# Expert slots weighted one at a time, key choices cut into pieces, and gathered rows in the weight ring

## The chip, the cores and the metric

One core of one Trainium2 chip runs the whole program in one launch. The metric is the time of the program on the device in microseconds, the median of the runs shown; smaller is better.

## What is computed

A first block (two hybrid layers) and a second block (two layers) follow each other on 256 tokens of width 1024. The change concerns the second block, whose layer is this:

```python
xn = rmsnorm(x, norm_mix[l])
proj = xn @ w_in[l]                      # five mixers read slices of it
cat = rmsnorm(cat, group_norm[l])        # the mixers' outputs
x = x + cat @ w_out[l]
x = x + peer_ffn(rmsnorm(x, norm_ffn[l]), peer_wq[l], peer_subkeys[l], peer_u[l], peer_v[l])

def peer_ffn(xn, wq, subkeys, u_tab, v_tab):
    q = (xn @ wq).reshape(b, s, 8, 2, 128)
    sc = einsum('bshjc,hjkc->bshjk', q, subkeys)
    top_s, top_i = top_k(sc, 16)
    cand = top_s[..., 0, :, None] + top_s[..., 1, None, :]
    best, ci = top_k(cand, 16)
    idx = i1 * 128 + i2                  # which of 16384 experts
    g = softmax(best)
    act = gelu(einsum('ckd,cd->ck', u_tab[idx], xn))
    y = einsum('ck,ckd->cd', g * act, v_tab[idx])
```

Each token takes 8 heads x 16 = 128 experts. An expert is a row of 2048 floats, u beside v, in one table in HBM.

## The kernel before

Tokens lie in two tiles of 128 (`tt` 0 and 1). `second` (L1424) runs for each layer `mix2` (five mixers, then `down`, the product with w_out), then `peer`. The program is built with the tile framework's scheduler, which may move an engine's instructions past each other; `issue_after` keeps a step from being placed before a given instruction. Each engine then runs its own list strictly in order.

**Weights.** `unit` (L196) loads 1 MB into one of three `raw` buffers of the ring (L188) and splits it in two halves: ScalarE rounds to `hi` (L212), VectorE or GpSimd makes `lo = raw - hi` (L216). A product is three matmuls (L236).

**The expert stage.** `peer` (L1248) first takes in the mixers' output (`arrive`, L1256: the sum, the gain, the transposes), projects head 0 and 1 for tile 0 (`project`, L1298) and chooses experts (`route`, L1321: `top16` by VectorE's max, index and replace instructions, then index arithmetic, some 35 VectorE instructions a head and tile, and one exponential on ScalarE). Then come 256 *slots*: 16 for each of 8 heads, first all of tile 0 ("first half"), then all of tile 1 ("second half"). For a slot, GpSimd issues an indirect DMA (L1377) that gathers 128 rows of 8 KB, 1 MB, into one of 8 `uv` buffers; VectorE multiplies the u half with the token and sums (L1379, the *dot*); ScalarE makes the gelu (L1383), VectorE multiplies by the gate (L1384), ScalarE scales an identity by the weight (L1387, `dgw`), and TensorE adds the weighted v half into two PSUM banks (L1389, two matmuls that the profile shows as four records). Then the buffer is free for the gather eight slots later. Four slots form a group: one gelu and one gate product for four weights.

```python
for i in range(GROUP):
    ... indirect_dma_start(out=r, ...)                     # L1377
    dots.append(... scalar_tensor_tensor(..., accum_out=act[:, i:i + 1]))
nc.scalar.activation(wt, act, AF.Gelu, scale=rs[tt])       # 128 x 4
nc.vector.tensor_tensor(wt, wt, gate[:, tt, h, k0:k0 + GROUP], op=OP.mult)
for i, r in enumerate(rows):
    nc.scalar.activation(dg, self.ident, AF.Copy, scale=wt[:, i:i + 1])
    for half in range(2): nc.tensor.matmul(y[tt][half], dg, r[:, ...])
```

The rest of the layer's routing is put between the groups by a list `todo`: the second token tile's `arrive`, the projections of heads 2 to 7 (each brings a wq unit), and a `route` for each head and tile. Each is one step, which the scheduler may then spread. After `peer`, `add_rms` (L1234) adds the result, normalizes and transposes for the next layer, whose first product (`attention(0)` in `mix2`, tile `p_s2`) begins.

Of the kernel before, what the change touches and what calls it, by code (L numbers as in the profile page):

```python
# [47 lines left out]
GROUP = 4  # L48
# [127 lines left out]
class _Kernel:  # L176
# [75 lines left out]
    def toks_first(self, outs, ws, xt):  # L252

        for tt in range(NT):
            k0, n = 0, sum(len(w[0]) for w in ws)
            for w in ws:
                for k in range(len(w[0])):
                    self.mm3(outs[tt], [t[:, tt, k0] for t in xt], [t[k] for t in w], k0 == 0, k0 == n - 1)
                    k0 += 1
# [140 lines left out]
    def down(self, y, unit, n, lhs, at, places=(None, None), parts=2):  # L400
# [561 lines left out]
    def mix2(self, l, x, xt):  # L962
# [33 lines left out]
        def attention(c):  # L996
            p = [self.bank([512], "acc", "p_s2") for _ in range(NT)]
            self.toks_first(p, [self.unit(a["win2_s"][l, c, kh], 4, 512, 8 if c == 0 else 0) for kh in range(2)], xt)
# [150 lines left out]
        self.down(y, lambda b, **k: self.unit(a["wout2"][l, order[b]], 2, D, LO, **k), len(order),  # L1149
                  lambda b: self.cat[order[b]], lambda b: 0, (None, place))  # L1150
# [95 lines left out]
    def peer(self, l, x, xt, y_in):  # L1246
# [9 lines left out]
        def arrive(tt):  # L1256
# [4 lines left out]
            for i in range(2):  # L1261
# [3 lines left out]
                self.transposed(xg[tt][:, sl], KT // 2, xt, tt, k0=i * KT // 2)  # L1265
            for i in range(2):
# [54 lines left out]
        def route(tt, h):  # L1321
# [14 lines left out]
            top16(c, best, ci)  # L1336
            ids = W.tile([P, 2, TOPK], F32, tag="ids", name="ids", bufs=2)
# [12 lines left out]
            nc.vector.tensor_tensor(cf, cf, i1, op=OP.subtract)  # L1350
            for j, (pos, out) in enumerate(((ab, i1), (cf, i2))):
# [15 lines left out]
            return last  # L1367
# [3 lines left out]
        def experts(tt, h, k0):  # L1371

            rows = []
            act = W.tile([P, GROUP], F32, tag="act", name="act", bufs=3)
            for i in range(GROUP):
                r = uv.pop(0) if uv else W.tile([P, 2 * D], F32, tag="uv", name="uv", bufs=GBUFS)
                nc.gpsimd.indirect_dma_start(out=r, out_offset=None, in_=a["puv"],  # L1377
                                             in_offset=bass.IndirectOffsetOnAxis(ap=idx[:, tt, h, k0 + i:k0 + i + 1], axis=0))
                dots.append(nc.vector.scalar_tensor_tensor(r[:, :D], r[:, :D], 1.0, xg[tt], op0=OP.mult, op1=OP.mult,  # L1379
                                                           accum_out=act[:, i:i + 1]))  # L1380
                rows.append(r)
            wt = W.tile([P, GROUP], F32, tag="wt", name="wt", bufs=3)
            nc.scalar.activation(wt, act, AF.Gelu, scale=rs[tt])  # L1383
            nc.vector.tensor_tensor(wt, wt, gate[:, tt, h, k0:k0 + GROUP], op=OP.mult)  # L1384
            for i, r in enumerate(rows):
                dg = W.tile([P, P], F32, tag="dgw", name="dgw", bufs=4)
                nc.scalar.activation(dg, self.ident, AF.Copy, scale=wt[:, i:i + 1])  # L1387
                for half in range(2):
                    nc.tensor.matmul(y[tt][half], dg, r[:, D + 512 * half:D + 512 * half + 512],  # L1389
                                     start=h == 0 and k0 + i == 0, stop=h == HEADS - 1 and k0 + i == TOPK - 1)  # L1390


        weights(0)
        arrive(0)
        project(0, 0, 1)
        dots = [route(0, 0)]
        weights(1)
        project(1, 0, 1)

        def late():  # L1400
            arrive(1)
            if l + 1 < L:
# [11 lines left out]
        for n, (tt, h) in enumerate([(tt, h) for tt in range(NT) for h in range(HEADS)]):  # L1414
            for k0 in range(0, TOPK, GROUP):
                while todo and todo[0][0] <= TOPK * n + k0:
                    step = todo.pop(0)[1]
                    with self.tc.issue_after(dots[-1].ins):
                        step()
                experts(tt, h, k0)  # L1420
# [57 lines left out]
```

## Time and profile before

| | |
|---|---|
| median of 3 runs | 3249.17 us (3243.63 to 3259.98) |
| profiled execution, its own time | 3238.84 us |
| span of its instructions | 3237.1 us |
| TensorE busy | 87% of the span |
| VectorE, ScalarE, GpSimd busy | 66%, 37%, 27% |
| mean granted TensorE clock | 0.94 |
| bytes moved by DMA | 841.78 MB, mean 260 GB/s |
| software DMA queue (the gathers) | 536.90 MB |
| expert gathers issued, first and last of layer 0 | 1606.99 us, 2327.01 us |
| expert gathers issued, first and last of layer 1 | 2515.05 us, 3213.80 us |

The shares are averages over stages with different limits, so the page's total says little: the span is to be read in stretches. A 40-slice strip on the page and the views by stretch give each stretch its busy engines, its granted clock and what the DMA engines moved. A wait in brackets behind an instruction is the idle time of its engine just before, and what ended it.

### The profile page before, as it was taken

How to read it: one execution, taken by the hardware profiler on the slowest of the kernel's cores; microseconds unless marked ns; L12 is line 12 of the kernel's file. 1: busy time of each engine (PE TensorE's matmuls, PEld its weight loads, DVE VectorE, ACT ScalarE, POOL GpSimd, SP SyncE). 2: the span in 40 equal slices, each digit the busy share in tenths (PEclk: the TensorE clock that was granted, in tenths of full speed). 3: DMA queues.
4: the chain of work that ended last, by engine and by line, in shares of the span. 5: the costliest groups of instructions: out<-in, count | busy, mean ns of one | idle time of the engine just before them, and what ended most of it. 6: DMA issues, size and time to landing. Idle time of an engine off the chain costs nothing.

```text
span 3237.1 us, 39712 instructions
## 1 busy us (share of the span) xinstructions
PE 2814.0 (87%) x13968; PEld 2058.1 (64%) x13968; DVE 2131.9 (66%) x4974; ACT 1199.3 (37%) x2300; POOL 882.7 (27%) x628
## 2 busy tenths in 40 slices
PE   9999999999999999999788877777889688867777
PEld 9988988989988988978644433332377344323333
DVE  6568667565577567569766676666487666766664
ACT  5446344445445344436432222212164322222121
POOL 0013221011023220011234454434311444444343
PEclk9999999999999999999889988888899899898889
DMA  6554235555553344554399999999843899999998
GB/s 256 183 187 158 100 122 202 183 182 213 182 189 135 105 156 176 182 184 144 129 379 397 391 371 365 397 378 374 344 146 108 347 391 376 378 399 384 379 376 353
DMA packets 121734, 841.78 MB, mean 260 GB/s; under 512 B 14016, under 2 KB 16832, under 8 KB 22208
## 3 DMA queue, kind: packets, MB, share of 16 engines
q0 software_dynamic: 73728, 536.90, 41.4%
q1 hardware_dynamic: 47520, 301.82, 26.2%
q8 instruction: 111, 1.82, 0.2%
q14 instruction: 87, 0.71, 0.1%
q10 hardware_dynamic: 288, 0.52, 0.0%
HBM read 838.15 MB, written 1.05 MB: 259 GB/s over the span
## 4 chain that ended last, share of the span: by engine, by line
PE 46%; DMA 19%; DVE 17%; issue 9%; POOL 6%; ACT 2%; POOLq 0%; DVEq 0%; SPq 0%; ACTq 0%
DMA uv<-in_puv_dram,idx 19%; PE p_gu L236 14%; PE p_y L236 10%; POOL uv L1377 6%; DVE uv L1379 4%; PE p_g L236 4%; PE p_y L1389 3%; PE p_b L236 2%; PE p_c L236 2%; PE p_gx L236 2%; DVE conv L542 1%; DVE lo L216 1%; PE p_tr L293 1%; PE p_s L236 1%; ACT hi L212 1%
## 5 line engine op out<-in xcount | busy, mean ns | idle before, releaser
L1389 PE MATMUL p_y<-uv,dgw 128*128 128x512 f32 x2048 | 1024.9, 659 | 295.8 <-ACT dgw L1387 295.8
L1389 PEld LDWEIGHTS p_y<-uv,dgw 128*128 128x128 f32 x2048 | 423.5, 212 | 866.5 <-issue 498.8
L1379 DVE SCALAR_TENSOR_TENSOR uv<-uv,xg 128x1024 f32<-128x1024 f32 x512 | 632.6, 1237 | 479.4 <-DMA uv<-in_puv_dram,idx 448.4
L1377 POOL DMA_INDIRECT uv<-in_puv_dram,idx x512 | 603.1, 1178 | 870.9 <-PE p_y L1389 508.3
L216 DVE TENSOR_TENSOR lo<-raw,hi 128x1024 fp32r<-128x1024 f32 (+1 forms) x390 | 480.7, 1236 | 311.9 <-ACT hi L212 309.9
L212 ACT CAST hi<-raw 128x1024 fp32r<-128x1024 f32 (+1 forms) x500 | 513.8, 1034 | 449.4 <-PE p_gu L236 125.1
L216 POOL TENSOR_TENSOR lo<-raw,hi 128x1024 fp32r<-128x1024 f32 (+1 forms) x110 | 274.4, 2500 | 1446.6 <-ACT hi L212 860.1
L236 PE MATMUL p_gu<-xt,hi 128*128 128x256 f32 x2560 | 463.6, 283 | 0.0
L236 PEld LDWEIGHTS p_gu<-xt,hi 128*128 128x128 f32 x2560 | 399.6, 192 | 0.0
L236 PE MATMUL p_gu<-xt,lo 128*128 128x256 f32 x1280 | 362.5, 283 | 0.0
L1383 ACT ACTIVATE wt<-act,rms_r 128x4 f32<-128x4 f32 x128 | 38.1, 297 | 848.2 <-DVE uv L1379 848.1
L236 PEld LDWEIGHTS p_gu<-xt,lo 128*128 128x128 f32 x1280 | 245.7, 192 | 0.0
L1387 ACT ACTIVATE dgw<-ident,wt 128x128 f32<-128x128 f32 x512 | 165.6, 391 | 77.6 <-DVE wt L1384 65.3
L236 PE MATMUL p_c<-xt,hi 128*128 128x256 f32 x960 | 182.6, 290 | 0.4 <-ACT sh L1095 0.4
L236 PE MATMUL p_y<-hi,ht 128*128 128x512 f32 x576 | 181.2, 395 | 0.0
L236 PEld LDWEIGHTS p_c<-xt,hi 128*128 128x128 f32 x960 | 152.9, 194 | 2.4 <-ACT sh L1095 1.1
L236 PE MATMUL p_c<-xt,lo 128*128 128x256 f32 x480 | 138.2, 289 | 0.0
L236 PE MATMUL p_y<-lo,ht 128*128 128x512 f32 x320 | 126.3, 395 | 0.0
L236 PE MATMUL p_g<-hi,xt 128*128 128x512 f32 x384 | 125.1, 399 | 0.0
L236 PEld LDWEIGHTS p_y<-hi,ht 128*128 128x128 f32 x576 | 108.5, 188 | 25.1
L236 PEld LDWEIGHTS p_c<-xt,lo 128*128 128x128 f32 x480 | 92.9, 194 | 0.2
L236 PE MATMUL p_g<-lo,xt 128*128 128x512 f32 x192 | 77.3, 403 | 8.2 <-DVE lo L216 7.0
(517 smaller groups left out, 3953.0 us busy)
## 6 DMA issues: line engine op xcount, KB each, us to landing
raw<-in_gu_dram SPq DMA_DIRECT2D x86, 1024.0 KB, 4.8
raw<-in_dn_dram SPq DMA_DIRECT2D x44, 1024.0 KB, 4.8
raw<-in_win_t_dram SPq DMA_DIRECT2D x30, 1024.0 KB, 4.9
raw<-in_win_g_dram SPq DMA_DIRECT2D x24, 1024.0 KB, 4.8
raw<-in_wout_dram SPq DMA_DIRECT2D x18, 1024.0 KB, 4.9
raw<-in_wq_dram SPq DMA_DIRECT2D x16, 1024.0 KB, 4.9
raw<-in_wbr_dram SPq DMA_DIRECT2D x12, 1024.0 KB, 4.8
raw<-in_win_s_dram SPq DMA_DIRECT2D x8, 1024.0 KB, 8.1
```

Of the source, the lines that this page charges most:

```text
L212: self.nc.scalar.copy(hi, r)
L216: engine.tensor_tensor(lo[:, a:b], r[:, a:b], hi[:, a:b].bitcast(F32), op=OP.subtract)
L236: self.nc.tensor.matmul(out, A[i], B[j], start=first and n == 0, stop=last and n == 2)
L293: nc.tensor.transpose(p[:, j], x[:, (g + j) * P:(g + j + 1) * P], self.ident)
L542: nc.vector.scalar_tensor_tensor(c[:, s:], th[:, j, :T - s], pc[:, 4 * f + 3 - s:4 * f + 4 - s], c[:, s:], op0=OP.mult, op1=OP.add)
L1377: nc.gpsimd.indirect_dma_start(out=r, out_offset=None, in_=a["puv"], in_offset=bass.IndirectOffsetOnAxis(ap=idx[:, tt, h, k0 + i:k0 + i + ...
L1379: dots.append(nc.vector.scalar_tensor_tensor(r[:, :D], r[:, :D], 1.0, xg[tt], op0=OP.mult, op1=OP.mult, accum_out=act[:, i:i + 1]))
L1383: nc.scalar.activation(wt, act, AF.Gelu, scale=rs[tt])
L1387: nc.scalar.activation(dg, self.ident, AF.Copy, scale=wt[:, i:i + 1])
L1389: nc.tensor.matmul(y[tt][half], dg, r[:, D + 512 * half:D + 512 * half + 512], start=h == 0 and k0 + i == 0, stop=h == HEADS - 1 and k0 + ...
```

## The change

- Each slot has its own gelu (128 x 1); the product with the gate moves from VectorE to ScalarE (a Copy with the gate as its scale); the groups of four are gone, and with them the VectorE product.
- `route` and `arrive` become generators that yield between pieces (six pieces a `route`). Behind every dot, `beside` lets one piece of the first due step run. The due slots move a little (for tile 1 from 24 to 20 slots ahead). The choice of head 1, tile 0, is made before the first slot.
- In the second half, slots 0, 4 and 7 of every 11 gather into the ring's three `raw` buffers instead of a `uv` buffer, in layer 0 up to slot 107 of 128, in layer 1 to the end.
- wq's first unit is asked for inside `down`, before the last products of the mixers (`then`), and not in `peer`.
- The next layer's `add_rms` for tile 0, its two first units and the first product for tile 0 are written as a step due at slot 228 (`following`), and `attention(0)` goes on from there.

```diff
@@ down, mix2
         last = [(m + i, unit(m + i, place=place, parts=parts)) for i, place in enumerate(places)]
+        if then:
+            then()
...
+        def then():
+            self.wq0 = self.unit(a["wq"][l, 0], KT, 2 * P)
@@ attention
+            if c == 0 and l:
+                ws, p0 = self.begun
+                p = [p0, self.bank([512], "acc", "p_s2")]
+                self.tile_toks(p[1], ws, xt, 1)
@@ route
             for j in range(2):
                 top16(sc[:, j], tv[:, j], ti[:, j])
+                yield
...
             top16(c, best, ci)
+            yield
...
             nc.vector.tensor_tensor(cf, cf, i1, op=OP.subtract)
+            yield
...
                 nc.vector.tensor_reduce(out, e, axis=AX.X, op=OP.add)
+                if j == 0:
+                    yield
@@ expert (was experts, by groups)
+        def expert(tt, h, k):
+            n = TOPK * h + k
+            if uv:
+                r = uv.pop(0)
+            elif tt == NT - 1 and n % 11 in (0, 4, 7) and n < (108 if l + 1 < L else 128):
+                r = self.ring.tile([P, 2 * D], F32, tag="raw", name="raw", bufs=3)
+            else:
+                r = W.tile([P, 2 * D], F32, tag="uv", name="uv", bufs=GBUFS)
...
+            dot = nc.vector.scalar_tensor_tensor(r[:, :D], r[:, :D], 1.0, xg[tt], ..., accum_out=act)
+            dots.append(dot)
+            beside(dot)
             nc.scalar.activation(wt, act, AF.Gelu, scale=rs[tt])
-            nc.vector.tensor_tensor(wt, wt, gate[:, tt, h, k0:k0 + GROUP], op=OP.mult)
+            nc.scalar.activation(wt, wt, AF.Copy, scale=gate[:, tt, h, k:k + 1])
+            dg = W.tile([P, P], F32, tag="dgw", name="dgw", bufs=4)
+            nc.scalar.activation(dg, self.ident, AF.Copy, scale=wt)
@@ following
+        def following():
+            self.next_xt = self.xt_tiles()
+            self.add_rms(x, y, self.next_xt, 0)
+            yield
+            ws = []
+            for kh in range(2):
+                ws.append(self.unit(a["win2_s"][l + 1, 0, kh], 4, 512))
+                yield
+            p = self.bank([512], "acc", "p_s2")
+            self.tile_toks(p, ws, self.next_xt, 0)
+            self.begun = ws, p
+            yield
@@ the list of steps
-            todo.append((TOPK * (HEADS + h) - 24, lambda h=h: route(1, h)))
+            todo.append((TOPK * (HEADS + h) - 20, route(1, h)))
+        if l + 1 < L:
+            todo.append((TOPK * (2 * HEADS - 2) + 4, following()))
...
+        def beside(dot):
+            if todo and todo[0][0] <= len(dots) - 2:
+                with self.tc.issue_after(dot.ins):
+                    while todo and next(todo[0][1], todo) is todo:
+                        todo.pop(0)
```

How the built programs' instructions stand, at three places. An x at a row's end counts repeats.

ScalarE in the first half of layer 0, about slots 16 to 23 (`act` holds dots, `wt` the weights, `dgw` the scaled identity). Before:

```order
L1383 ACTIVATE wt<-act,rms_r 128x4
L1387 ACTIVATE dgw<-ident,wt 128x128 x4
L1383 ACTIVATE wt<-act,rms_r 128x4
L1387 ACTIVATE dgw<-ident,wt 128x128 x4
L1383 ACTIVATE wt<-act,rms_r 128x4
```

Now:

```order
L1406 ACTIVATE wt<-act,rms_r 128x1
L1407 ACTIVATE wt<-wt,gate_15641 128x1
L1409 ACTIVATE dgw<-ident,wt 128x128
L1406 ACTIVATE wt<-act,rms_r 128x1
L1407 ACTIVATE wt<-wt,gate_15641 128x1
L1409 ACTIVATE dgw<-ident,wt 128x128
```

A weight waits for one dot and not for four, and VectorE is no longer between gelu and `dgw`.

VectorE at the same place, where the choice of head 2 begins. Before:

```order
L1379 SCALAR_TENSOR_TENSOR uv,act<-uv,xg_15635 128x1024 x4
L1275 MAX tv<-sc 128x8 x2
L1276 MAX_INDEX ti<-tv,sc 128x8
L1384 TENSOR_TENSOR wt<-wt,gate_15631 128x4
L1276 MAX_INDEX ti<-tv,sc 128x8
L1332 TENSOR_TENSOR cand<-tv 128x24
L1277 MATCH_REPLACE sc<-tv,sc 128x128 x2
L1278 MAX tv<-sc 128x8 x2
L1279 MAX_INDEX ti<-tv,sc 128x8
L1332 TENSOR_TENSOR cand<-tv 128x36
L1379 SCALAR_TENSOR_TENSOR uv,act<-uv,xg_15635 128x1024
```

Now:

```order
L1403 SCALAR_TENSOR_TENSOR uv,act<-uv,xg_15645 128x1024 x8
L1288 MAX tv<-sc 128x8
L1289 MAX_INDEX ti<-tv,sc 128x8
L1290 MATCH_REPLACE sc<-tv,sc 128x128
L1291 MAX tv<-sc 128x8
L1292 MAX_INDEX ti<-tv,sc 128x8
L1403 SCALAR_TENSOR_TENSOR uv,act<-uv,xg_15645 128x1024
L1288 MAX tv<-sc 128x8
L1289 MAX_INDEX ti<-tv,sc 128x8
```

The scheduler had put dots between the instructions of a choice already, at places of its own; now there is a dot after every piece.

VectorE between the mixers' last product and the experts of layer 0 (`p_y` is that product, `xg` the input times the gain, the second `lo` rows the first wq units). Before:

```order
L216 TENSOR_TENSOR lo<-raw,hi 128x1024 x2
L1263 TENSOR_TENSOR x_74<-p_y,x_74 128x512 x2
L296 TENSOR_TENSOR cat_1_15402<-p_tr,cat_0_15401 128x256
L216 TENSOR_TENSOR lo<-raw,hi 128x1024 x2
L1264 TENSOR_TENSOR xg_15635<-x_74,gain 128x512 x2
```

Now:

```order
L215 TENSOR_TENSOR lo<-raw,hi 128x1024 x2
L1275 TENSOR_TENSOR x_74<-p_y,x_74 128x512 x2
L298 TENSOR_TENSOR cat_1_15402<-p_tr,cat_0_15401 128x256
L215 TENSOR_TENSOR lo<-raw,hi 128x1024 x2
L1276 TENSOR_TENSOR xg_15645<-x_74,gain 128x512 x2
```

Nothing moved here but the line numbers; TensorE, ScalarE and SyncE stand as before up to the first slot too. The four `lo` of the next layer's first two units, on GpSimd behind gathers 96 and 100 of layer 0 before, are VectorE's now, behind dot 231. The next layer's `add_rms` for tile 0 and its product `p_s2` stood behind dot 131 of layer 0 before (the scheduler had drawn them forward) and stand behind dots 229 to 231 now.

## Rows read from the trace of the kernel before

**Rows 1.** The page's strip of 40 slices of the span: DMA share in tenths, GB/s.

```profile
DMA  6554235555553344554399999999843899999998
GB/s 256 183 187 158 100 122 202 183 182 213 182 189 135 105 156 176 182 184 144 129 379 397 391 371 365 397 378 374 344 146 108 347 391 376 378 399 384 379 376 353
```

**Rows 2.** Busy time by stretch of the expert stages; last columns clock, DMA share, GB/s.

```profile
core 0: us, PE busy (x) PEld busy (x) DVE busy (x) ACT busy (x) POOL busy (x), PEclk, DMA share, GB/s
1612.00:2332.00 720.00, 561.75 (x1431) 265.02 (x1432) 459.19 (x1310) 173.03 (x424) 308.16 (x256) 0.87 0.96 383
...
2523.00:3220.00 697.00, 538.06 (x1402) 253.70 (x1403) 446.76 (x1292) 165.92 (x413) 294.28 (x250) 0.90 0.96 388
3160.00:3220.00 60.00, 45.16 (x98) 18.63 (x98) 30.57 (x54) 9.45 (x30) 24.97 (x24) 0.96 1.01 424
...
1690.00:1980.00 290.00, 233.65 (x672) 116.86 (x671) 196.26 (x577) 76.78 (x178) 127.81 (x103) 0.89 0.96 387
1980.00:2332.00 352.00, 269.38 (x546) 114.33 (x545) 212.70 (x597) 71.36 (x190) 148.35 (x128) 0.86 0.95 379
...
2900.00:3160.00 260.00, 190.95 (x375) 79.32 (x374) 166.17 (x508) 56.30 (x144) 108.21 (x94) 0.86 0.95 382
```

**Rows 3.** Timeline of 1999 to 2018 us, layer 0, while an expert choice is made.

```profile
1999.53 9.32 PE L1389 MATMUL p_y<-uv,dgw 128*128 128x512 f32 x16 [4.71 <-ACT dgw L1387]
...
2001.39 0.33 PEld L1389 LDWEIGHTS p_y<-uv,dgw 128*128 128x128 f32 x1 [0.52 <-issue]
...
2003.58 0.94 POOL L1377 DMA_INDIRECT uv<-in_puv_dram,idx  x1 [6.74 <-DVE uv L1379]
...
2017.95 1.62 POOL L1377 DMA_INDIRECT uv<-in_puv_dram,idx  x1 [7.65 <-PE p_y L1389]
```

**Rows 4.** The stretch 2000 to 2020 us alone, columns as in rows 2.

```profile
2000.00:2020.00 20.00, 19.76 (x58) 10.64 (x58) 16.20 (x58) 5.87 (x13) 6.25 (x6) 0.90 0.83 335
```

**Rows 5.** Timeline of one group of four slots late in layer 1, no choice running.

```profile
3187.01 1.23 DVE L1379 SCALAR_TENSOR_TENSOR uv<-uv,xg 128x1024 f32<-128x1024 f32 x1 [0.67 <-DMA uv<-in_puv_dram,idx]
...
3194.31 1.25 DVE L1379 SCALAR_TENSOR_TENSOR uv<-uv,xg 128x1024 f32<-128x1024 f32 x1 [1.20 <-DMA uv<-in_puv_dram,idx]
...
3195.60 0.30 ACT L1383 ACTIVATE wt<-act,rms_r 128x4 f32<-128x4 f32 x1 [7.88 <-DVE uv L1379]
...
3196.64 7.13 PE L1389 MATMUL p_y<-uv,dgw 128*128 128x512 f32 x16 [2.61 <-ACT dgw L1387]
...
3198.90 0.94 POOL L1377 DMA_INDIRECT uv<-in_puv_dram,idx  x1 [3.66 <-PE p_y L1389]
...
3204.05 0.94 POOL L1377 DMA_INDIRECT uv<-in_puv_dram,idx  x1 [0.37 <-PE p_y L1389]
```

**Rows 6.** The gathers' time from issue to landing, all 512 of them.

```profile
DMA to landing us min/median/max: 5.5/9.1/15.2
```

**Rows 7.** Groups of instructions, 1690 to 1980 us: busy, mean ns, idle before.

```profile
L1384 DVE TENSOR_TENSOR wt<-wt,gate 128x4 f32<-128x4 f32 x25 | 3.8, 154 | 2.6 <-ACT wt L1383 2.6
...
L1387 ACT ACTIVATE dgw<-ident,wt 128x128 f32<-128x128 f32 x100 | 32.2, 390 | 20.5 <-DVE wt L1384 19.0 <-PE p_y L1389 1.1 <-PE p_q L236 0.3
...
L1383 ACT ACTIVATE wt<-act,rms_r 128x4 f32<-128x4 f32 x25 | 7.4, 297 | 153.7 <-DVE uv L1379 153.7
```

**Rows 8.** Stretch 1690 to 1980 us, instructions on `p_y` alone: PE, PEld, DVE busy.

```profile
1690.00:1980.00 290.00, 201.11 (x396) 82.62 (x395) 0.00 (x0) 0.89 0.96 387
```

**Rows 9.** Timeline of layer 1's end: last dot, then the sum with x.

```profile
3223.70 1.23 DVE L1379 SCALAR_TENSOR_TENSOR uv<-uv,xg 128x1024 f32<-128x1024 f32 x1 [1.21 <-DMA uv<-in_puv_dram,idx]
...
3226.01 7.13 PE L1389 MATMUL p_y<-uv,dgw 128*128 128x512 f32 x16 [1.25 <-ACT dgw L1387]
3232.32 0.69 DVE L1447 TENSOR_TENSOR x<-p_y,x 128x512 f32<-128x512 f32 x1 [6.86 <-PE p_y L1389]
```

**Rows 10.** Chain of waits, mixers to experts, layer 0: start, us, what.

```profile
1585.46 2.36 DVE lo L216 x2
```

**Rows 11.** GpSimd's timeline at the stage's start: the ninth gather of layer 0.

```profile
1628.96 0.94 POOL L1377 DMA_INDIRECT uv<-in_puv_dram,idx  x1 [10.40 <-DVE rms_r L284]
```

More of the change, by code (lines that the diff above doesn't have):

```diff
@@ L254, in toks_first, with tile_toks @@
         for tt in range(NT):
[L255 to L259, printed above, removed]
+            self.tile_toks(outs[tt], ws, xt, tt)
+    def tile_toks(self, out, ws, xt, tt):
+        k0, n = 0, sum(len(w[0]) for w in ws)
+        for w in ws:
+            for k in range(len(w[0])):
+                self.mm3(out, [t[:, tt, k0] for t in xt], [t[k] for t in w], k0 == 0, k0 == n - 1)
+                k0 += 1
     def cols_first(self, name, ws, xt):
@@ L398, in ffn, with down @@
         return y
-    def down(self, y, unit, n, lhs, at, places=(None, None), parts=2):
+    def down(self, y, unit, n, lhs, at, places=(None, None), parts=2, then=None):
         def part(b, w, tts, hs):
@@ L996, in attention @@
         def attention(c):
-            p = [self.bank([512], "acc", "p_s2") for _ in range(NT)]
-            self.toks_first(p, [self.unit(a["win2_s"][l, c, kh], 4, 512, 8 if c == 0 else 0) for kh in range(2)], xt)
+            if c == 0 and l:
[3 more added lines that the diff above has]
+            else:
+                p = [self.bank([512], "acc", "p_s2") for _ in range(NT)]
+                self.toks_first(p, [self.unit(a["win2_s"][l, c, kh], 4, 512, 8 if c == 0 else 0) for kh in range(2)], xt)
             for tt in range(NT):
@@ L1149, in mix2 @@
         self.down(y, lambda b, **k: self.unit(a["wout2"][l, order[b]], 2, D, LO, **k), len(order),
-                  lambda b: self.cat[order[b]], lambda b: 0, (None, place))
+                  lambda b: self.cat[order[b]], lambda b: 0, (None, place), then=then)
         return y
@@ L1366, in route @@
             nc.vector.tensor_scalar(g, g, z, None, op0=OP.mult)
-            return last
         y = [[self.bank([512], "acc", "p_y") for _ in range(2)] for _ in range(NT)]
[L1371 to L1382, printed above, removed]
-            nc.scalar.activation(wt, act, AF.Gelu, scale=rs[tt])
-            nc.vector.tensor_tensor(wt, wt, gate[:, tt, h, k0:k0 + GROUP], op=OP.mult)
[L1385 to L1390, printed above, removed]
@@ L1393, in peer, with at_once @@
+        def at_once(steps):
+            for _ in steps:
+                pass
+        dots = []
         weights(0)
-        arrive(0)
+        at_once(arrive(0))
         project(0, 0, 1)
-        dots = [route(0, 0)]
+        at_once(route(0, 0))
         weights(1)
         project(1, 0, 1)
+        with self.tc.issue_after(dots[0].ins):
+            at_once(route(0, 1))
         def late():
-            arrive(1)
+            yield from arrive(1)
             if l + 1 < L:
                 self.load_gain(l + 1)
-            project(0, 1)
-            project(1, 1)
@@ L1413, in peer @@
         todo.sort(key=lambda t: t[0])
[L1414 to L1420, printed above, removed]
+        def beside(dot):
[3 more added lines that the diff above has]
+                        todo.pop(0)
+                        if not todo or todo[0][0] > len(dots) - 2:
+                            break
@@ L1421, in peer @@
+        for tt in range(NT):
+            for h in range(HEADS):
+                for k in range(TOPK):
+                    expert(tt, h, k)
         assert not todo
@@ L1435, in second @@
                 if l + 1 < L:
-                    xt = self.xt_tiles()
-                    for tt in range(NT):
-                        self.add_rms(x, y, xt, tt)
+                    xt = self.next_xt
+                    self.add_rms(x, y, xt, 1)
                 else:
```

26 lines of the change are left out of this document (21 added, 5 removed).

## The prediction

> **What bounds the kernel now.** The page's strip first [rows 1]: from slice 20 the DMA engines are 0.8 to 1.0 busy for nine slices, and again for the last nine; those are the two expert stages, some 1420 of 3237 us. Next the busy time by stretch [rows 2]: there TensorE is busy 78%, VectorE 64%, ScalarE 24%, and the DMA engines 0.96 of the time at 383 and 388 GB/s. The reader should compare this with the last 60 us of layer 1, when all choices have been made: 424 GB/s, DMA share 1.01 [rows 2]. A gather is 1.0486 MB, so it takes the DMA engines 2.47 us when they never run dry. The same bytes at 424 GB/s would need 720 x 383 / 424 = 650 us in layer 0 and 697 x 388 / 424 = 638 us in layer 1: **70 and 59 us** are lost to empty DMA queues.
>
> The timeline of a choice shows how [rows 3]: TensorE waits 4.71 us for a `dgw`, and GpSimd stands 6.74 and then 7.65 us before it may issue a gather, because no buffer is free; the 20 us around it move 335 GB/s at a share of 0.83 [rows 4]. The ring of 8 buffers lasts 8 x 2.47 = 19.8 us. How much of that is used up is read from a quiet group [rows 5]: its first dot starts at 3187.01, the fourth at 3194.31, the common gelu at 3195.60, the matmuls of all four slots at 3196.64, and the buffers go back to GpSimd from 3198.90 (first) to 3204.05 (fourth). So a buffer is held 11.9 us (first slot) to 9.7 us after its dot has begun. With the shortest landing of 5.5 us [rows 6] that is 17.4 us of 19.8: 2.4 us of slack. Any delay above it empties the queue. The expert stages are bound by DMA, but through this slack.
>
> **The change part by part.** Sums are against the profiled execution's 3238.84 us, 10 us under the median of 3249.17; savings are subtracted from the median.
>
> *Slots alone.* Gone: a layer's 64 gelus and 64 VectorE products (154 ns each [rows 7]) for four weights. New per slot on ScalarE: a gelu and a Copy of 128 x 1. Neither is in the trace; the nearest rows are the gelu of 128 x 4, 297 ns, and `dgw`, 390 ns [rows 7]. Below zero they can't cost, since they are added work; above `dgw` they hardly go, since they write less. I take 0.30 each. ScalarE's work per slot is then 0.30 + 0.30 + 0.39 = 1.0 us of 2.47, beside the DMA. On the chain of one slot the gelu to matmul stretch stays near 1.04 us [rows 5], as the VectorE step in it becomes a ScalarE step. A slot is then held from dot to first matmul 3196.64 - 3194.31 = 2.33 us, and from there to the buffer's return 2.26 us: 4.6 us in place of 9.7 to 11.9. Slack: 19.8 - 5.5 - 4.6 = **9.7 us**, four times as much.
>
> *Rows in the weight ring.* In the second halves 11 buffers last 27.2 us, slack 17.1 us. The ring's loads are idle then, apart from the next layer's. The destination's price is not in the trace; rows of the same 8 KB into other buffers give me no reason for one, so 0, and at most the 2% kept below.
>
> *Choices in pieces.* The same VectorE instructions, so no time by themselves. Six pieces over six slots in place of the scheduler's own spread. They delay a dot by a few microseconds at a time; the pauses they made, 6.74 and 7.65 us [rows 3], are below the new slack.
>
> *Does another engine become the bound?* TensorE in 1690 to 1980 us: 233.65 us busy, 201.11 of it on `p_y` [rows 2, 8], so 32.5 us for five projections, 6.5 a head; a slot is 7.13 / 4 = 1.78 us [rows 5]. A head of the first half is 16 x 1.78 + 6.5 = 35.0 us of TensorE. The DMA needs 16 x 2.47 + 2.8 (a wq unit and its keys, 1.18 MB) = 42.3 us. So 83%, and 72% in the second half. VectorE's 196.26 us of that stretch [rows 2], less 3.8 [rows 7], in some 270 us is 71%. DMA stays the bound.
>
> *wq's first unit.* Before and now VectorE makes that unit's `lo` between the sum and the gain product, in the same order; the other engines too stand as before. The step does not do what it says. Two `lo` there take 2.36 us on the chain [rows 10]; that bounds it at 2.4 us a layer either way, and I take 0.
>
> *The next layer's product.* It stood inside layer 0's expert stage already and still does; it moves from slot 131 to 231. Its four `lo` move from GpSimd to VectorE: 4.9 us by the `lo` of rows 10 (2.36 for two), in one block with sum and norm, some 10 us in which no dot runs. It holds two of the three ring buffers, so the slack there is between 9.7 and 17.1. Bounds 0 to 10 us; I take 5, for layer 0.
>
> *What stays lost.* Start: gather nine went out at 1628.96, after 10.40 us of waiting for the first group [rows 11], while the eight before it keep the DMA busy 19.8 us; it will go earlier, but TensorE is busy with tile 1's projections then: I take 4 us a layer. First halves, slack 9.7 against a choice and a projection that can meet: 7 us a layer, about 2.5%. Second halves: 0. Layer 0 keeps 16 of its 70 us, layer 1 keeps 11 of 59: **54 + 48 = 102 us** saved. Bounds: 129 us if nothing stays lost, about 45 if only some of the second halves is won (rival one).
>
> *Ends.* Last dot to the sum with x: 3232.32 - 3223.70 = 8.6 us [rows 9]; the matmuls of four slots stand in between, of which three will be done. Then 2.33 and two records of 0.45 with their end, 1.1, are 3.4 us: **5 us a layer**, 10 in all.
>
> Sum: 102 + 10 = 112. 3249 - 112 = **3137 us**; for the profiled execution 3127.
>
> **A page that speaks against it.** The expert stages already move 383 and 388 GB/s over 700 us each [rows 2]. The Trainium skill, *DMA: Bandwidth & Descriptors*, section Bandwidth, says that for transfers between HBM and SBUF the HBM side binds, near 358 GB/s a core; by that rule nothing is left to win here. The trace disagrees so far: 424 GB/s over 60 us. (The same section also lists 425 GB/s for one 16 MB transfer on a lone core.)
>
> **The rivals.**
> One, *only the second halves gain* (0.22). In the first halves wq loads, projections and choices meet on TensorE at 83% and on eight buffers. For it: the first halves run at 387, so they lose less than the second's 379 and 382, and a TensorE below full clock (0.89 there) comes near 42 us a head. Against it: slack fourfold. The second halves alone: 352 x (1 - 379/424) = 37 and 260 x (1 - 382/424) = 26, with the ends 73 us: 3176.
>
> Two, *the DMA engines have no more to give* (0.08). 424 GB/s would be what queues reach after or between pauses, and 385 what 700 us can bear. Only the ends are won: 3239, no change. For it: two stages with different pauses agree within 2%; this is where the page's rule would lead. Against it: 60 us without a dip.
>
> Three, *slower: TensorE stays at its lower clock in the second halves* (0.04). Groups gave it 7 us bursts; single slots give 1.8 us bursts with gaps. At the lower level a record takes 0.33 + 0.52 = 0.85 us [rows 3], a slot 3.4 us, above the DMA's 2.47, so TensorE would set the pace: 128 x 3.4 = 435 in place of 352 us, +83 a layer, less the first halves' gain of about 49: 3249 + 166 - 49 = 3366. It decides where the mean granted clock there falls under 1.78 / 2.75 = 0.65. Against it: 0.96 was granted in the evenest stretch, 0.83 to 0.86 only with 3 to 5 us waits [rows 2, 3].
>
> **How the numbers follow.** My forecast 0.66, own range 3110 to 3170. Faster by over 0.5% (16 us, about what a measurement of this kernel can tell from no change): forecast and rival one, 0.88. Same: rival two, 0.08. Slower: rival three, 0.04. The range goes from all 139 us won (3110) to rival one with a third of its 63 us missing (3249 - 42 - 10 = 3197, so 3200); it leaves out rivals two and three and a little of one, 0.16.
>
> **What would show it.** Right: 410 GB/s or more over each expert stage, DMA share 1.0 in the second halves, GpSimd's waits there no longer 7 us, ScalarE's three instructions a slot near 1 us, last dot to sum under 4 us, granted clock above 0.95 in the second halves. Wrong: stages still near 388 GB/s though the share is 1.0 (rival two); first halves unchanged with TensorE above 90% (rival one); records of 0.85 us through the second halves (rival three); a pause over 10 us near slot 231, where rows for slots 103 and 106 of the second half wait for the next layer's units.

## The result, and the profile after

| | before | after |
|---|---|---|
| median | 3246.66 us, 4 runs (3243.63 to 3259.98) | 3114.22 us, 4 runs (3111.29 to 3116.52) |
| ratio, 95% interval | | 0.9584 [0.9555, 0.9613] |
| profiled execution, span | 3238.84 us, 3237.1 us | 3116.52 us, 3114.8 us |
| mean granted TensorE clock | 0.940 | 0.975 |

The forecast was 3137 us (3110 to 3200), faster. The kernel is 4.2% faster, and the time lies in the range, near its lower end.

The page's strip of the changed kernel, DMA share in tenths and GB/s, to be laid beside [rows 1]:

```profile
DMA  6545325555555234555259999999962699999998
GB/s 252 189 159 186 115 82 197 200 191 204 184 180 181 105 109 162 198 188 205 82 189 424 427 424 427 427 427 427 370 247 82 256 426 415 427 427 426 427 427 344
```

The full slices of the expert stages stand at 415 to 427 GB/s, most of them at 427, where 365 to 399 stood, apart from one dip (370). By stretch, the halves of both layers (columns of [rows 2]; last three: granted clock, DMA share, GB/s):

```profile
core 0: us, PE busy (x) PEld busy (x) DVE busy (x) ACT busy (x) POOL busy (x), PEclk, DMA share, GB/s
...
1617.00:1940.00 323.00, 272.62 (x888) 137.21 (x888) 231.60 (x636) 161.46 (x436) 148.15 (x130) 0.97 1.01 425
1940.00:2281.00 341.00, 267.44 (x563) 102.58 (x564) 232.09 (x630) 157.53 (x437) 151.84 (x124) 0.96 0.99 413
...
2456.00:2780.00 324.00, 274.93 (x888) 137.93 (x888) 232.50 (x638) 161.50 (x436) 147.94 (x130) 0.96 1.01 423
2780.00:3100.00 320.00, 255.88 (x524) 93.59 (x524) 221.54 (x609) 150.26 (x423) 158.09 (x124) 0.98 1.01 424
```

Only the second half of layer 0 is not at a share of 1.01. Where the time went, stretch by stretch, from the first gather and the last dot of each layer. The lines of the changed kernel's timeline:

```profile
1613.58 1.09 POOL L1400 DMA_INDIRECT uv<-in_puv_dram,idx  x1 [33.47 <-DVE tv L1288]
...
2282.17 1.23 DVE L1403 SCALAR_TENSOR_TENSOR uv<-uv,xg 128x1024 f32<-128x1024 f32 x1 [1.19 <-ACT dgw L1409]
...
2452.80 0.95 POOL L1400 DMA_INDIRECT uv<-in_puv_dram,idx  x1 [33.43 <-DVE tv L1288]
...
3106.47 1.23 DVE L1403 SCALAR_TENSOR_TENSOR uv<-uv,xg 128x1024 f32<-128x1024 f32 x1 [1.19 <-ACT dgw L1409]
3108.85 1.99 PE L1411 MATMUL p_y<-uv,dgw 128*128 128x512 f32 x4 [0.44 <-ACT dgw L1409]
3110.01 0.69 DVE L1502 TENSOR_TENSOR x<-p_y,x 128x512 f32<-128x512 f32 x1 [2.31 <-PE p_y L1411]
```

Of the kernel before, the gathers' first times stand in the table ahead of the prediction and layer 1's last dot in [rows 9]; layer 0's last dot is this line:

```profile
2338.16 1.23 DVE L1379 SCALAR_TENSOR_TENSOR uv<-uv,xg 128x1024 f32<-128x1024 f32 x1 [1.17 <-DMA uv<-in_puv_dram,idx]
```

| stretch, us | before | after | difference | forecast |
|---|---|---|---|---|
| start to first gather | 1606.99 | 1613.58 | +6.6 | 0 |
| layer 0, first gather to last dot | 731.2 | 668.6 | -62.6 | -54 |
| last dot to layer 1's first gather | 176.9 | 170.6 | -6.3 | -5 |
| layer 1, first gather to last dot | 708.7 | 653.7 | -55.0 | -48 |
| last dot to the end of the span | 13.4 | 8.3 | -5.1 | -5 |
| sum | 3237.1 | 3114.8 | -122.3 | -112 |

The first row is no work of the change: before the first slot the engines' lists are the same, and the runs below, which all have these lists, issue their first gather between 1607.13 (e9) and 1615.52 us (e5). The changed kernel itself, run again as e12, issues it at 1609.46.

### The profile page after: what moved, and what is told of

Same layout as the page of the kernel before. It is cut to its first block, busy times and chain, and to the rows that moved or that the text cites. A ratio compares the mean times of both kernels' runs of the same rounds, so it can differ in the third digit from the quotient of the medians.

```text
span 3114.8 us, 40467 instructions
## 1 busy us (share of the span) xinstructions
PE 2776.7 (89%) x13968; PEld 2008.4 (64%) x13968; DVE 2138.2 (69%) x4850; ACT 1490.6 (48%) x3196; POOL 881.7 (28%) x624
## 4 chain that ended last, share of the span: by engine, by line
PE 49%; DMA 24%; DVE 19%; issue 4%; ACT 3%; POOL 1%; POOLq 0%; DVEq 0%; SPq 0%; ACTq 0%
DMA uv<-in_puv_dram,idx 19%; PE p_gu L235 15%; PE p_y L235 10%; DVE uv L1403 5%; DMA raw<-in_puv_dram,idx 4%; PE p_g L235 4%; PE p_y L1411 2%; PE p_b L235 2%; PE p_c L235 2%; PE p_gx L235 2%; PE p_s L235 1%; DVE conv L546 1%; POOL uv L1400 1%; PE p_q L235 1%; DVE lo L215 1%
## 5 line engine op out<-in xcount | busy, mean ns | idle before, releaser
L1411 PE MATMUL p_y<-uv,dgw 128*128 128x512 f32 x1788 | 862.2, 619 | 216.9 <-ACT dgw L1409 183.8
L1411 PEld LDWEIGHTS p_y<-uv,dgw 128*128 128x128 f32 x1788 | 323.7, 194 | 714.1 <-ACT dgw L1409 394.8
L1403 DVE SCALAR_TENSOR_TENSOR uv<-uv,xg 128x1024 f32<-128x1024 f32 x447 | 542.4, 1221 | 282.2 <-DMA uv<-in_puv_dram,idx 138.8
L1400 POOL DMA_INDIRECT uv<-in_puv_dram,idx x447 | 528.4, 1182 | 673.1 <-PE p_y L1411 289.6
L215 POOL TENSOR_TENSOR lo<-raw,hi 128x1024 fp32r<-128x1024 f32 (+1 forms) x106 | 265.1, 2506 | 1446.5 <-ACT hi L211 859.2
L1406 ACT ACTIVATE wt<-act,rms_r 128x1 f32<-128x1 f32 x512 | 150.3, 294 | 573.2 <-DVE uv L1403 469.8
L1409 ACT ACTIVATE dgw<-ident,wt 128x128 f32<-128x128 f32 x512 | 205.1, 400 | 16.9 <-PE p_y L1411 1.8
L1411 PE MATMUL p_y<-raw,dgw 128*128 128x512 f32 x260 | 134.0, 640 | 43.6 <-ACT dgw L1409 43.6
L1407 ACT ACTIVATE wt<-wt,gate 128x1 f32<-128x1 f32 x512 | 150.7, 294 | 16.0
L1411 PEld LDWEIGHTS p_y<-raw,dgw 128*128 128x128 f32 x260 | 47.6, 198 | 124.8 <-ACT dgw L1409 85.6
```

The source lines that it names most:

```text
L215: engine.tensor_tensor(lo[:, a:b], r[:, a:b], hi[:, a:b].bitcast(F32), op=OP.subtract)
L1403: dot = nc.vector.scalar_tensor_tensor(r[:, :D], r[:, :D], 1.0, xg[tt], op0=OP.mult, op1=OP.mult, accum_out=act)
L1407: nc.scalar.activation(wt, wt, AF.Copy, scale=gate[:, tt, h, k:k + 1])
L1409: nc.scalar.activation(dg, self.ident, AF.Copy, scale=wt)
```

## The experiments

Theory A: a gather goes out when its buffer is back, so what counts is the ring's length in time less landing less holding (slack); groups of four held each buffer 10 to 12 us, single slots 4.6. Theory B: the long blocks of choices on VectorE emptied the queue, and the pieces cured it. Theory C: the three more buffers of the second halves did. Each run stands against the kernel before on the same chip.

**e1_groups**, the changed kernel with groups of four again.

```diff
...
-            nc.scalar.activation(wt, act, AF.Gelu, scale=rs[tt])
-            nc.scalar.activation(wt, wt, AF.Copy, scale=gate[:, tt, h, k:k + 1])
+            if k % 4 < 3:
+                return
+            nc.scalar.activation(wt, act, AF.Gelu, scale=rs[tt])            # 128 x 4
+            nc.vector.tensor_tensor(wt, wt, gate[:, tt, h, k - 3:k + 1], op=OP.mult)
+            for i, r in enumerate(group[1:]):
                 ...
```

> The changed kernel, but four slots are weighted together again (one gelu of 128 x 4, one product on VectorE, then four dgw and eight matmul records); choices stay in pieces, rows stay in the weight ring. Theory A (slack: what counts is how long a buffer is held against how long the ring lasts): a buffer is held 9.7 to 11.9 us from its dot again, so the first halves with 8 buffers are back at 2.4 us of slack and fall from 425 to about 390 GB/s, some 27 us a layer, while the second halves with 11 buffers keep 9.8 us of slack and stay above 415 GB/s; the ends give back 5 us a layer. 3114 + 54 + 10 = 3178 us. Theory B (pieces: long blocks of choices on VectorE emptied the queue): the pieces are still there, only the ends give back: 3124 us. Theory C (ring: three more buffers did it): first halves as in A, no more.

Measured: 3210.81 us, ratio 0.9889 [0.9871, 0.9907]. Of the gain only 38 us (3248.99 to 3210.81) are left. B falls with it (3124 expected), as the pieces are still there. C is not told from A here, as both let the first halves fall back. A's 3178 was 33 us too low. Two stretches of layer 0 show where (first half, then most of the second):

```profile
1640.00:2020.00 380.00, 310.18 (x895) 155.19 (x894) 244.59 (x699) 95.48 (x229) 155.34 (x134) 0.88 0.95 372
2020.00:2290.00 270.00, 213.49 (x451) 91.87 (x449) 188.65 (x542) 65.31 (x163) 112.24 (x102) 0.90 0.98 413
```

With 11 buffers the groups do nearly well (413 GB/s), with 8 they don't (372), as A says; but 372 is below the 387 of [rows 2] with the same 8 buffers.

**e2_no_ring**, the three lines that take `raw` buffers for rows are out.

```diff
-            elif tt == NT - 1 and n % 11 in (0, 4, 7) and n < (108 if l + 1 < L else 128):
-                r = self.ring.tile([P, 2 * D], F32, tag="raw", name="raw", bufs=3)
```

> The changed kernel, but no row goes into the weight ring: 8 buffers in both halves. Theory A: the second halves get the 9.7 us of slack that the first halves already have, and those moved 425 GB/s with it, so nothing is lost there; the pause of some 30 us near slot 231, where a row for the ring stood behind the next layer's units, goes: 3104 to 3114 us. Theory C: the second halves fall back to 380 to 390 GB/s, some 30 us a layer: about 3165 us. Theory B: 3104 to 3114 us, as A.

Measured: 3109.32 us, 0.9566 [0.9549, 0.9583]. C falls (3165 expected): eight buffers carry the second halves nearly as well as the first, at 421 GB/s (1935 to 2260 and 2770 to 3095 us). The strip, second halves in slices 26 to 29 and 36 to 39:

```profile
GB/s 260 182 169 176 116 84 197 202 192 200 185 180 179 107 109 163 197 190 206 82 192 424 426 427 427 427 413 425 420 216 84 259 426 419 423 427 427 427 425 351
```

**e3_whole_choices**, each choice as one step behind one dot, not in forced pieces.

```diff
-            todo += [... (TOPK * h - 14, route(0, h))]
+            todo += [... (TOPK * h - 14, whole(route(0, h)))]    # runs all pieces behind one dot
-            todo.append((TOPK * (HEADS + h) - 20, route(1, h)))
+            todo.append((TOPK * (HEADS + h) - 20, whole(route(1, h))))
```

> The changed kernel, but each choice is made in one block behind one dot instead of in pieces over six slots. Theory A: a choice makes a pause of some 7 us for the queue, less than the 9.7 and 17.1 us of slack, so the stages stay above 415 GB/s: 3114 to 3125 us. Theory B: the pauses empty the queue as before, 30 choices of a few us each: 3160 us or more.

Measured: 3112.68 us, 0.9584 [0.9568, 0.96]. No difference to the change. But the edit does not make the block that both expectations speak of: the scheduler puts dots between a choice's instructions again, as it did in the kernel before. A choice of this run, its first instruction, the first of the four dots inside it, and its last instruction:

```profile
1898.50 0.48 DVE L1288 MAX8 tv<-sc 128x8 f32<-128x128 f32 x2
...
1900.77 1.22 DVE L1403 SCALAR_TENSOR_TENSOR uv<-uv,xg 128x1024 f32<-128x1024 f32 x1
...
1911.29 0.18 DVE L1376 TENSOR_SCALAR idx<-i 128x16 uint32<-128x16 f32 x1
```

So the run shows that forced pieces gain nothing over the scheduler's own spread. With e4 below, which has that spread too and the whole gain, B falls. What a true block would cost was not tried.

**e4_before_slots_alone**, the kernel before with groups of one, nothing else of the change.

```diff
-GROUP = 4
+GROUP = 1
...
-        todo = [(0, lambda: route(0, 1)), (GROUP, late)]
+        todo = [(0, lambda: route(0, 1)), (4, late)]
-            act = W.tile([P, GROUP], F32, tag="act", name="act", bufs=3)
+            act = W.tile([P, GROUP], F32, tag="act", name="act", bufs=4)
```

(`wt` likewise gets four buffers. Steps of `todo` can now begin at any slot and not only at every fourth.)

> The kernel before with one part of the change alone: groups of one slot (gelu of 128 x 1, the product with the gate on VectorE, one dgw), 8 buffers, choices where the scheduler puts them. Theory A: slack 9.7 us in both halves, so nearly all of the queue's loss is won and the ends with it: about 3247 - 115 - 10 = 3122 us, and at most 3140. Theory B: the choices still stop the dots in one block, less than half is won: 3190 us or more. Theory C: only what the first halves can give without a ring of 11: about 3190 us too, with the second halves at 380 to 390 GB/s.

Measured: 3111.59 us, 0.9576 [0.956, 0.9592]: **this one part is the whole gain.** The product with the gate stays on VectorE here, and the chain of a slot is no longer for it. Timeline of the end: last dot, gate product, sum:

```profile
3100.96 1.23 DVE L1379 SCALAR_TENSOR_TENSOR uv<-uv,xg 128x1024 f32<-128x1024 f32 x1 [0.61 <-DMA uv<-in_puv_dram,idx]
...
3102.61 0.16 DVE L1384 TENSOR_TENSOR wt<-wt,gate 128x1 f32<-128x1 f32 x1 [0.42 <-ACT wt L1383]
3104.48 0.69 DVE L1447 TENSOR_TENSOR x<-p_y,x 128x512 f32<-128x512 f32 x1 [1.71 <-PE p_y L1389]
```

From dot to sum 3.52 us, with ScalarE's product 3.54 (3106.47 to 3110.01): which engine multiplies by the gate is of no account.

**e5_five_buffers**, e2 with `GBUFS = 5`. It turns the slack back without touching how slots are weighted.

```diff
-GBUFS = 8
+GBUFS = 5
```

> The kernel of run e2_no_ring (the changed kernel, no rows in the weight ring) with 5 buffers in place of 8. Theory A (slack alone): 5 x 2.46 = 12.3 us of ring, less 5.5 us of landing and 4.6 us from dot to return, are 2.2 us of slack, what the kernel before had with 8 buffers and groups of four (2.4 us). Then both stages fall back to 350 to 390 GB/s and the time to 3220 us or more, though every slot is weighted alone. Theory D (the four returns at once, not the time held, starved the queue): with single returns 5 buffers lose little: 3110 to 3140 us.

Measured: 3236.99 us, 0.9969 [0.9951, 0.9987]. From first gather to last dot its two layers take 724.8 and 718.0 us, together as long as the 731.2 and 708.7 of the kernel before within 3 us: in the stages five buffers with single slots are as slow as eight with groups of four, as the slack of 2.2 and 2.4 us says, and what is left of the gain is about what the ends give. D falls. A quiet stretch late in layer 1 of this run shows the holding time itself, since a gather here waits for the buffer of the slot just done:

```profile
3198.99 1.23 DVE L1400 SCALAR_TENSOR_TENSOR uv<-uv,xg 128x1024 f32<-128x1024 f32 x1 [1.20 <-ACT dgw L1406]
...
3201.36 1.98 PE L1408 MATMUL p_y<-uv,dgw 128*128 128x512 f32 x4 [0.45 <-ACT dgw L1406]
...
3203.62 0.94 POOL L1397 DMA_INDIRECT uv<-in_puv_dram,idx  x1 [1.49 <-PE p_y L1408]
```

Dot to matmul 2.37 us (forecast 2.33), dot to the next gather 4.63 us (forecast 4.6).

**e6_groups_whole_choices**, e1 and e3 together.

```diff
...
+            if k % 4 < 3:
+                return
...
+            todo += [... (TOPK * h - 14, whole(route(0, h)))]
```

> The kernel of run e1_groups (four slots weighted together, ring kept) with each choice in one block instead of in pieces: of the three parts about the stage only the rows in the weight ring are left. Run e1_groups was slower in its first halves (349 to 386 GB/s) than the kernel before (some 387). If the pieces themselves cost there, since each of six slots then gets its dot later while a group of four waits for its last one, this run is faster than 3211 us: first halves at 385 GB/s, 3160 to 3190 us. If the spread of a choice over slots is harmless and it was chance of order, it stays at 3200 to 3215 us.

Measured: 3200.51 us, 0.9861 [0.9832, 0.9889]. That is the lower edge of the second expectation, and the interval overlaps that of e1. As in e3 the scheduler spreads the choices, so no block is tried, and whether forced pieces cost something where groups are kept isn't settled.

**e7_ring_to_100**, one number.

```diff
-            elif tt == NT - 1 and n % 11 in (0, 4, 7) and n < (108 if l + 1 < L else 128):
+            elif tt == NT - 1 and n % 11 in (0, 4, 7) and n < (100 if l + 1 < L else 128):
```

> The changed kernel with one number changed: in layer 0 rows go into the weight ring only up to slot 99 of the second half instead of 107, so slots 103 and 106 use ordinary buffers and their gathers are not behind the next layer's two units. If that order makes the pause near slot 231 (340, 247 and 271 GB/s over 30 us, some 10 us of transfer lost), it goes and the time falls to 3103 to 3107 us. If VectorE's block there (sum, norm and four lo, 10 us without a dot) makes it, the pause stays and the time is 3112 to 3116 us.

Measured: 3107.38 us, 0.9572 [0.9548, 0.9596]. The pause it aims at, in the changed kernel, by stretch and in GpSimd's and VectorE's timelines:

```profile
2220.00:2230.00 10.00, 3.07 (x6) 1.19 (x5) 3.53 (x6) 2.97 (x9) 0.00 (x0) 0.65 0.80 340
2230.00:2240.00 10.00, 5.66 (x10) 2.10 (x8) 2.26 (x3) 0.93 (x3) 1.88 (x2) 0.84 0.74 247
2240.00:2250.00 10.00, 9.88 (x19) 4.35 (x20) 8.18 (x16) 7.26 (x24) 3.14 (x3) 0.83 0.72 271
```

```profile
2205.44 0.94 POOL L1400 DMA_INDIRECT raw<-in_puv_dram,idx  x1 [2.37 <-PE p_y L1411]
...
2216.04 0.94 POOL L1400 DMA_INDIRECT raw<-in_puv_dram,idx  x1 [0.59 <-DVE lo L215]
2234.22 0.94 POOL L1400 DMA_INDIRECT uv<-in_puv_dram,idx  x1 [17.25 <-PE p_y L1411]
...
2224.89 1.23 DVE L1403 SCALAR_TENSOR_TENSOR raw<-raw,xg 128x1024 f32<-128x1024 f32 x1 [6.25 <-DMA raw<-in_puv_dram,idx]
...
2237.74 1.23 DVE L1403 SCALAR_TENSOR_TENSOR raw<-raw,xg 128x1024 f32<-128x1024 f32 x1 [9.33 <-DMA raw<-in_puv_dram,idx]
```

Two rows go out late. Slot 103's goes out at 2205.44, after that of slot 109: two `raw` buffers are taken by the units, and it needs the third, which slot 99 has until then. Slot 106's goes out at 2216.04, after that of slot 112, because its `raw` buffer holds a unit until the `lo` is made. Dots run in slot order, so VectorE waits 6.25 us for the one row and 9.33 us for the other. The rows behind them keep their buffers meanwhile, those of slots 107 to 112 to the end, and GpSimd stands 17.25 us. In e7 the same stretches read:

```profile
2220.00:2230.00 10.00, 7.63 (x21) 3.57 (x20) 4.23 (x9) 3.97 (x12) 4.80 (x4) 1.00 1.01 428
2230.00:2240.00 10.00, 7.55 (x16) 2.54 (x16) 5.17 (x9) 3.96 (x12) 3.30 (x4) 1.00 1.01 427
2240.00:2250.00 10.00, 8.17 (x18) 2.72 (x17) 5.12 (x9) 3.96 (x12) 3.99 (x5) 1.00 1.01 424
```

The pause is gone, while VectorE still makes the sum, the norm and the four `lo`, with two dots now between the pairs of `lo`. That speaks for the order of the gathers as its cause; the block by itself was not tried. The times do not separate e7 from the change (e12).

**e8_no_early_product**, `following` taken out.

```diff
-            if c == 0 and l:
+            if False:
...
-            todo.append((TOPK * (2 * HEADS - 2) + 4, following()))
...
-                    xt = self.next_xt
-                    self.add_rms(x, y, xt, 1)
+                    xt = self.xt_tiles()
+                    for tt in range(NT):
+                        self.add_rms(x, y, xt, tt)
```

> The changed kernel with the next layer's first product left where the kernel before has it (sum, norm and transposes of tile 0 and the units wherever the scheduler puts them, in the first part of the second half; the code of the early product is taken out). If the early product gains by being late (my term: it costs 5 us through its block on VectorE and the two ring buffers it holds), this kernel is 5 to 10 us faster, 3104 to 3109 us; if its point is that the layer's end gets shorter, it is slower by up to 5 us, 3114 to 3120 us.

Measured: 3111.94 us, 0.9586 [0.9562, 0.9609]: no difference that can be told. Neither expectation is borne out.

**e9_six_buffers**, e2 with `GBUFS = 6`.

```diff
-GBUFS = 8
+GBUFS = 6
```

> The kernel of run e2_no_ring with 6 buffers in place of 8. Theory A (slack alone, in a straight line): 6 x 2.46 less 10.1 us are 4.7 us of slack, between the 2.2 us of five buffers (3237 us) and the 9.7 us of eight (3109 us): on the line between them 3194 us. Rival: the pauses that reach the queue are those of 2 to 5 us that five buffers showed (GpSimd's waits for p_y, longest 4.9 us), so 4.7 us of slack already covers nearly all of them: 3110 to 3140 us.

Measured: 3150.61 us, 0.9716 [0.9687, 0.9745]. Between both expectations: the loss falls faster with slack than a line, but 4.7 us do not cover all. Layer 0's stretch 1640 to 1960 us, in this order: the kernel before (8 buffers, groups, slack 2.4 us), e5 (5 buffers, 2.2), e9 (6 buffers, 4.7), e2 (8 buffers, 9.7):

```profile
1640.00:1960.00 320.00, 263.27 (x788) 134.45 (x787) 209.44 (x598) 86.29 (x199) 141.06 (x113) 0.90 0.96 384
```

```profile
1640.00:1960.00 320.00, 259.18 (x820) 124.47 (x818) 210.41 (x578) 152.72 (x403) 116.77 (x112) 0.98 0.98 387
```

```profile
1640.00:1960.00 320.00, 265.70 (x816) 126.92 (x814) 220.27 (x611) 155.58 (x415) 131.23 (x119) 0.98 0.99 407
```

```profile
1640.00:1960.00 320.00, 269.10 (x833) 129.08 (x832) 229.91 (x647) 161.34 (x433) 139.21 (x122) 0.99 1.01 426
```

The rate follows the slack, 384 and 387, 407, 426 GB/s, whichever way the slack was made.

**e10_five_whole_choices**, e5 and e3 together.

```diff
-GBUFS = 8
+GBUFS = 5
...
+            todo += [... (TOPK * h - 14, whole(route(0, h)))]
...
```

> The kernel of run e5_five_buffers (5 buffers, no rows in the weight ring) with each choice in one block. With eight buffers pieces or blocks made no difference (run e3_whole_choices). If pieces are worth something where slack is short, a block of some 7 us with 2.2 us of slack costs about 5 us for each of 30 choices, less what the pieces cost now: slower than 3237 us by 30 us or more. If what counts is the sum of VectorE's delay, however it is cut, the time stays at 3225 to 3245 us.

Measured: 3236.92 us, 0.9954 [0.9933, 0.9974], the time of e5: forced pieces gain nothing over the scheduler's spread even where slack is short. A block is not made here either.

**e11_no_hoist**, wq's first unit made in `peer` again.

```diff
-            w = self.unit(a["wq"][l, h], KT, 2 * P) if h else self.wq0
+            w = self.unit(a["wq"][l, h], KT, 2 * P)
```

> The changed kernel with wq's first unit made where the kernel before makes it. By my term the hoist moves no instruction: 3111 to 3116 us, no difference to the changed kernel. If it does shorten the head, this kernel is slower by up to 5 us (two layers of 2.4 us): 3116 to 3119 us.

Measured: 3110.41 us, 0.9582 [0.956, 0.9604]: no difference, as the equal lists had it.

**e12_change_again**, the change itself, no edit.

> The changed kernel itself, for a direct comparison with run e7_ring_to_100 (3107.4 us) and run e8_no_early_product (3111.9 us). If the pause near slot 231 costs what its slices show, some 10 us of transfer less what the other slots give back, it is 3112 to 3117 us; if the runs of e7 were only on a quicker day, 3107 to 3110 us.

Measured: 3110.97 us (3108.66 to 3115.87, 5 runs), 0.9591 [0.9568, 0.9614], between its two expectations, and its interval overlaps that of e7. Its profile shows the pause again (246, 274 and 356 GB/s from 2220 to 2250 us), and its layer 0 takes 653.1 us from first to last gather, e7's 649.5: the stage gains 3.6 us, which is too little for the times to tell. e7 is the fastest in the median, but not shown to beat the change.

## Why the prediction was right

**The bound.** Right, and shown: DMA queues running empty because buffers came back late. e4 adds only the shorter holding time and gains all; e1 takes only that away and loses most; e5 undoes the slack by another means, and its stages are as slow as before.

**Slots alone.** The price of the new ScalarE instructions, 0.30 us each, was 294 ns for either, and `dgw` stayed near its 390 ns of [rows 7]. Groups of the changed kernel, busy and mean ns:

```profile
L1409 ACT ACTIVATE dgw<-ident,wt 128x128 f32<-128x128 f32 x512 | 205.1, 400 | 16.9 <-PE p_y L1411 1.8
L1407 ACT ACTIVATE wt<-wt,gate 128x1 f32<-128x1 f32 x512 | 150.7, 294 | 16.0
L1406 ACT ACTIVATE wt<-act,rms_r 128x1 f32<-128x1 f32 x512 | 150.3, 294 | 573.2 <-DVE uv L1403 469.8 <-DVE raw L1403 93.7 <-issue 1.4
```

The Trainium skill, *ScalarE: Activation LUTs*, section What ACT_TABLE_LOAD costs, gives an instruction with a per-partition operand some 280 ns and 0.833 ns per element of a row. By that an estimate for these is 281 and 387 ns; the traces agree to some 13 ns, with 294 at one element and 400 at 128. The holding time, 4.6 us, was 4.63 (e5).

**Rows in the weight ring.** The need for them was wrong: with eight buffers and 9.7 us of slack (e2) a second half loses 325 x (1 - 421/427) = 4.6 us, where the changed kernel's loses 11.2 in layer 0 and 2.2 in layer 1. The step that gave the second halves' zero to eleven buffers failed; it changed no number, because single slots come close to that zero alone. No run measures the 17.1 us by itself.

**Choices in pieces** and **wq's first unit**: 0 forecast, 0 measured (e3 and e10, against the scheduler's own spread; e11).

**The other engines.** TensorE was forecast at 83% and 72%, VectorE at 71%. In the stretches above TensorE is busy 272.62 of 323 us (84%) in a first half, 267.44 of 341 (78%) and 255.88 of 320 (80%) in the second ones, VectorE 231.60 of 323 (72%). The miss in the second halves is the slot's price: four records by themselves take 1.98 us, not a quarter of the 7.13 us of sixteen [rows 5], 1.78. Still under 2.46 us of DMA, so it cost nothing.

**The next layer's product.** I took 5 us, between 0 and 10. The pause that I named among the signs of being wrong came, at the place that I named, and its three slices hold 30 x 427 - 10 x (340 + 247 + 271) = 4230 us x GB/s too little, 9.9 us of transfer. But e7 without it is only 3.6 us shorter in the stage than e12 with it. The rest comes back at the stage's end, as the stretches up to the last dot show (2274.06 in e7, 2277.55 in e12; first e7, then e12):

```profile
2260.00:2270.00 10.00, 8.13 (x17) 2.71 (x17) 5.12 (x9) 3.96 (x12) 0.02 (x1) 1.00 0.64 271
2270.00:2274.00 4.00, 3.05 (x7) 0.87 (x5) 1.65 (x4) 1.98 (x6) 0.00 (x0) 1.00 0.08 29
```

```profile
2260.00:2270.00 10.00, 8.09 (x17) 2.71 (x16) 4.99 (x8) 4.14 (x13) 1.87 (x2) 1.00 1.01 428
2270.00:2278.00 8.00, 6.42 (x13) 2.33 (x14) 4.15 (x7) 3.05 (x10) 0.00 (x0) 1.00 0.81 339
```

At 427 GB/s as the full rate e7 loses 7.4 us here and e12 1.6. With the 9.5 us of e12's own pause (246, 274 and 356 GB/s) that makes 9.5 + 1.6 - 7.4 = 3.7 us. From 2270 us e7 moves 29 GB/s, about a sixteenth of 427. Layer 1 of the changed kernel, which has no pause, ends alike, with 26 GB/s from 3100 to 3105 us, and its dot at 3101.62 has waited 2.20 us for its row. So one of the 16 DMA engines may fall behind the others in an even stretch and catch up in a pause. That is an estimate from these rates; no view here shows the engines singly. That my 5 us lie near the 3.6 is luck: I had the slack between 9.7 and 17.1 us while the units hold two ring buffers, and GpSimd stood 17.25 us.

**What stays lost, the term that was mis-sized.** At the 427 GB/s that whole slices reach, the kernel before lost 720 x (1 - 383/427) = 74 and 697 x (1 - 388/427) = 64 us [rows 2], 138 and not 129: the quiet stretch's 424 GB/s was taken for the full rate. The changed kernel loses 1.5 and 11.2 us in layer 0 (425 and 413 GB/s in 323 and 341 us) and 3.0 and 2.2 us in layer 1: 18 us where 27 were forecast. In layer 0's first half I had put 4 us for the start and 7 for meetings of choices and projections; both together were 1.5. The start was covered because the ninth gather no longer waits for a group, cf. [rows 11]:

```profile
1626.29 1.28 POOL L1400 DMA_INDIRECT uv<-in_puv_dram,idx  x1 [2.89 <-PE p_y L1411]
```

It goes out 12.7 us after the first, within the 19.8 us that eight gathers last. 138 - 18 = 120 us saved in the stages, 102 forecast: half of the difference is the full rate, half the losses. (By first gather and last dot the table above has 118.)

**Ends.** 8.6 us from last dot to sum [rows 9] were to become 3.4, and are 3.54: 5 us a layer, as forecast.

**The median.** The rest of the distance from 3137 to 3114 us is in the runs: the profiled execution of before lay 8 us under its median, that of the change 2 us above, so profiles differ by 122 us and medians by 132.

**The rivals.** One, only the second halves gain: no, the first halves run at 425 and 423 GB/s. Two, DMA has no more to give: no, 427 GB/s slice after slice. The Trainium skill, *DMA: Bandwidth & Descriptors*, section Bandwidth, has the HBM side bind near 358 GB/s a core; this case's traces disagree, while the 425 GB/s that the same section lists for a lone core are what the stages now reach. Three, TensorE at its lower clock: no, the granted clock is 0.96 to 0.98 in the stretches above where it was 0.86 to 0.89 [rows 2]. (The 0.83 that this rival gives as a clock is the DMA share of [rows 4]; the lowest clock in the rows is 0.86.)

## What to carry to other kernels

Where a ring of buffers feeds a stage that DMA should bound, work out its slack from one quiet stretch: buffers times the transfer's time, less landing, less the time from a buffer's first use to its return. Cut the holding time first: here that was worth 137 us (e4), with groups of one in place of four, while three more buffers for some of the rows, forced pieces of other work and moved products beside it were worth nothing that could be measured. Too few buffers undo it: five in place of eight took nearly all of it back (e5). A row that waits for a buffer of another ring stops every row behind it, since the consumer takes rows in order.

## What was not expected

- TensorE's clock was not by itself what held the stages back. e5 has the low rate of the kernel before (387 and 384 GB/s) at a granted clock of 0.98 in place of 0.90: single slots raise the clock, slack raises the rate. How much a lower clock adds where groups are kept, by longer matmuls, no run separates.
- Keeping the queue full makes each gather slower and the stage faster. From issue to landing the gathers into `uv` took 9.1 us in the median before [rows 6]; in e12, the changed kernel, 14.7:

```profile
DMA to landing us min/median/max: 5.4/14.7/24.7
```

- Groups of four with eight buffers ran slower in the changed program (372 GB/s, e1) than in the kernel before (387). The pieces are at most a part of it (e6, 379). e1 and e6 also begin their steps behind any dot, within a group too, where the kernel before begins them between groups; no run tries that by itself. This stays open.
